# Sums and splits of two x pairs interleaved in the first feed-forward periods, sums of steady periods moved, one query product made a filler

## The chip, the cores and the metric

The kernel runs on one core of a Trainium2 chip. The metric is the device time in microseconds of one execution of the whole program. Three executions of the kernel before gave 1489.28, 1490.77 and 1493.35 us; the median is 1490.77 us. PE stands for TensorE (matmuls), DVE for VectorE, ACT for ScalarE, POOL for GpSimd and SP for SyncE.

## The reference

The program is a two-layer encoder trunk over 512 frames and 16 meta tokens, of width 1024. Each layer is a mixer (retention in the first, latent attention in the second) and a SwiGLU feed-forward of hidden width 2816. What the change touches are the two feed-forwards and the query products of the second layer. Cut to that, the reference is:

```python
def swiglu(hn, w1, w3, w2):
    return (jax.nn.silu(hn @ w1) * (hn @ w3)) @ w2
...
    cq = rmsnorm(hn @ w_q_a, q_a_norm_g)
    q = (cq @ w_q_b).reshape(B, L, MLA_HEADS, MLA_NOPE + MLA_ROPE)
    ...
        sc = jnp.einsum('bqhd,bkhd->bhqk', q[:, s:e], k[:, :e])
...
    for layer in range(DEPTH):
        h = h + mixer(rmsnorm(h, norm_mix_g[layer]))
        h = h + swiglu(rmsnorm(h, norm_ffn_g[layer]), ffn_w1[layer], ffn_w3[layer], ffn_w2[layer])
    return rmsnorm(h, final_g)[:, PAD + N_META:]
```

All inputs are float32, and so is the result. Numbers are carried as a high and a low part: every 128-wide matmul step is three matmuls (high by high, high by low, low by high).

## The kernel before

**Splits.** `split(hi, lo, z)` (its two instructions are recorded at L335 and L331) is an ACT cast that writes the high part and a DVE subtraction that writes the low part. The subtraction reads what the cast wrote, so DVE cannot begin it before ACT has ended. Weights arrive by DMA in a tile `raw` and are split into `whi` and `wlo`; operands are split into `xp`. All plain DVE additions and subtractions are recorded at L331 too.

**The feed-forward.** `ffn(0, True)` works on 528 columns (two halves of w = 264), `ffn(1, False)` on 512 (two of 256). Both call `quads` (L812), which runs a list of *quads* in *periods*: eight `Up` quads (columns of w1 and w3), four `Down` quads (w2), then 6, 4, 8, 4 and 4. A quad is a 2x2 block product. Most quads are *mixed*: they take a Strassen-like scheme of seven products Q1 to Q7 instead of eight, each of four 128-wide steps, 12 matmuls. That needs sums and differences of the weight blocks (by DMAs that add while they write, `add1` and `add3` from POOL's queue, and by DVE, `sum2` and `sum4`) and of the operand blocks (four DVE operations `e<-e` in `operands`, L784). The first quads of each list (PLAIN = two in the first feed-forward, three in the second) and the last four are *plain*: eight products without any such sums, so they can start before the operands' sums exist.

**A mixed period** of quad q, with the next quad nxt and the one before prev, issues in this order (L909 to L995): product Q1; the split of group 2 of q's weights; an ACT copy of Q1's bank (L944); the hidden work of this period; Q7, Q3 and the recombination of prev; prev's evacuation `mid` (two DVE products `t<-a,r` and `t<-b,r`); `sum2(nxt)`, a DVE operation at L854; the split of q's third group; `sum4(nxt)`, a DVE subtraction `raw<-raw`; Q5; the split of group 1 of nxt, whose parts Q1 and Q5 of the next period read; Q2 and Q6; prev's SiLU on ACT; Q4 of prev; prev's `fin` on DVE. At the end of `quads` each engine's instructions are tied in this written order, so no scheduler changes it.

**Operands.** For the hidden units, `operands` runs in two half-steps, one per period (`hidden`, L1065): splits of three blocks and then the four `e<-e` in the first, the split of the four summed blocks `xp<-e,xp` in the second. A pair of `Up` quads makes one such operand, so a first half-step falls in every second period (a *heavy* one) and a second half-step in the periods between (*light* ones). For the four pairs of the input x, the first half-step runs with the mixer's last products (`prep_ffn`), and the rest, sums and split together, is in `self.sums`: a table `also` (L1039) says at which place of which period each runs. A place is a period and either "start", a number k (after the k-th step of period 0), "group2", "group1" or "end".

**The norm.** The feed-forward's RMS norm is applied after the first products. `root` (L1019) sums squares over partitions with two matmuls by ones (one for each half of the columns) into two free banks and takes their square roots on ACT (L1023); `inverse` (L1026) is a DVE reciprocal; `negated` (L1029) an ACT copy with the sign changed. `early` is `root` into the banks a1 and b1 of the second period. In the second feed-forward `squares` also makes the squares there (ACT) and their sum (DVE, `acc<-acc,t`).

**The second mixer** is placed by a scheduler from the program's order. The queries of each head are a product of 18 matmuls `query(n)` (L373) with a split after it; heads go through `scores`, `weights` and `values`, and between them a `Filler` runs as many pieces of other products as the table FILL says. Before the loop `query(0)` and `query(1)` are run to the end.

The main parts of the table and the loop:

```python
        drain(query(0))
        drain(query(1))
...
            cur.scores(0)
            filler.steps(FILL[n][0])
```

Of the kernel before, what the change touches and what calls it, by code (L numbers as in the profile page):

```python
# [52 lines left out]
A11, A21, A12, A22 = range(7, 11)  # L53
# [2 lines left out]
         "final": (40, 8), "kva": (48, 4), "qa": (52, 6), "gn": (58, 16)}  # L56
NG = 74

FILL = ((0, 0, 2, 1, 2), (2, 0, 2, 0, 1), (1, 0, 2, 2, 1), (1, 0, 1, 1, 2),
        (0, 1, 1, 1, 2), (1, 1, 1, 1, 2), (0, 1, 2, 2, 2), (0, 1, 0, 2, 2))  # L60


def drain(steps):
    for _ in steps:
        pass
# [195 lines left out]
class Kernel:  # L261
# [522 lines left out]
    def operands(self, pool, vv, w, b12=None):  # L784


        xp = pool.tile([P, 7, 2, HT], F32R, tag="xp", name=self.name("xp"))
        (b11, b12_), (b21, b22) = ((vv[:, i, :w], vv[:, i, w : 2 * w]) for i in range(2))
        for q, z in ((slice(Q1, Q3), vv[:, :, :w]), (Q3, b22)):
            self.split(xp[:, q, 0, :w], xp[:, q, 1, :w], z)  # L790
        if b12 is not None:
            self.split(*b12, b12_)
            yield xp
        self.tt(b11, b11, b12_, ALU.subtract)
        self.tt(b12_, b22, b12_, ALU.subtract)
        self.tt(b22, b22, b11, ALU.add)
        self.tt(b21, b22, b21, ALU.subtract)
        if b12 is None:
            yield xp
        self.split(xp[:, Q5:, 0, :w], xp[:, Q5:, 1, :w], self.blocks(vv, w))  # L800

    @staticmethod
# [9 lines left out]
    def quads(self, seq, first, w, ready, also, hidden):  # L812
# [3 lines left out]
        nc = self.nc  # L816
# [11 lines left out]
        def load1(q):  # L828
            q.r1 = f3(q, raw(q))
            nc.sync.dma_start(out=q.r1, in_=f3(q, q.src[:, : 2 * q.n]))  # L830
# [26 lines left out]
        def sum4(q):  # L857
            self.tt(q.r3[:, 1], q.r2[:, 1], q.r2[:, 0], ALU.subtract)
# [26 lines left out]
                    nc.tensor.matmul(bank, wt[u][:, cs], xp[:, p, v, :w], start=first and k == 0 and i == 0,  # L885
                                     stop=False, skip_group_check=True)

        def plain(q, j, k, rows=(0, 1)):

            cs = slice(k * P, (k + 1) * P)  # L890
            x1, x2 = q.blocks(k)[2 * j : 2 * j + 2]
            for row in rows:
                wt, banks = q.f[((A11, A12), (A21, A22))[row][j]], ((q.a, q.b), (q.d, q.c))[row]
                for bank, x in zip(banks, (x1, x2)):
                    for i, (u, v) in enumerate(((0, 0), (0, 1), (1, 0))):
                        nc.tensor.matmul(bank, wt[u][:, cs], x[v], start=j == 0 and k == 0 and i == 0,  # L896
                                         stop=False, skip_group_check=True)

        def begin():
            a, b = seq[:2]  # L900
# [8 lines left out]
        def period(i):  # L909
# [23 lines left out]
            if mixed(q):  # L933
                product(q, q.a, Q1, True)
            elif nxt:
                for k in pairs:
                    plain(q, 0, k)
            if q:
                group2(q)
                on("group2")  # L940
# [11 lines left out]
            if mixed(prev):  # L952
                product(prev, prev.d, Q7, False)
                product(prev, prev.b, Q3, False)
                combine(prev)
            prev.mid(prev.a, prev.b)
            if mixed(nxt):
                sum2(nxt)
            if mixed(q):
                group(q, q.r3, Q7, Q3)  # L960
            if mixed(far):
                load3(far)
            if mixed(nxt):
                sum4(nxt)
            if mixed(q):
                product(q, q.c, Q5, True)
            elif nxt:
                for k in pairs:
                    plain(q, 1, k)
            else:  # L970
                for row in range(2):
                    for k in pairs:
                        plain(q, 0, k, (row,))
                        plain(q, 1, k, (row,))
            if mixed(q):
                q.q5 = self.temp()[:, :w]
                nc.scalar.copy(out=q.q5, in_=q.c)
            if nxt:
                group1(nxt)
                if far:  # L980
                    load2(far)
                if i >= first - 1 and i + 3 < len(seq):
                    load1(seq[i + 3])
            on("group1")
            if mixed(q):
                product(q, q.a, Q2, False)
# [21 lines left out]
    def ffn(self, layer, full):  # L1008
# [25 lines left out]
                self.square_add(acc, self.h[k][:, META:], k == 0)  # L1034


        sums = [partial(drain, z) for z in self.sums]
        early = partial(root, (self.banks[1][0], self.banks[1][1][:, 0]))
        if full:  # L1039
            also = {(0, "start"): [sums[0]], (0, 1): [early, sums[1]], (0, 3): [inverse],  # L1040
                    (1, "group1"): [sums[2]], (1, "end"): [sums[3], negated]}
        else:
            also = {(0, "start"): [squares, sums[0]], (0, 3): [early], (1, "group2"): [inverse],
                    (1, "group1"): [sums[1]], (1, "end"): [negated], (2, "group1"): [sums[2]],
                    (2, "end"): [sums[3]]}

# [36 lines left out]
    def mla(self):  # L1085
# [83 lines left out]
        def query(n):  # L1169
            def evac(m, ps):  # L1170
                hi, lo = self.slot(F32R), self.slot(F32R)
                self.split(hi[:, :SEQ], lo[:, :SEQ], ps[:, :SEQ])
                qn[n] = hi, lo

            yield from self.gemm(a["w_qbn"], n, 1, cq, False, evac=evac)
# [35 lines left out]
        drain(rotary(0))  # L1211
        drain(second)
        drain(query(0))
        drain(query(1))


        order = {"q2": query(2), "q3": query(3), "r1": rotary(1), "q4": query(4), "kv2": keys_values(2), "p0": project([0], 0), "p0b": project([0], 1), "q5": query(5), "q6": query(6), "kv3": keys_values(3), "q7": query(7), "p1": project([1], 0), "p1b": project([1], 1), "p2": project([2], 0), "p2b": project([2], 1)}
        filler = Filler(order)
        prev = None
        for n in range(MH):  # L1220
# [177 lines left out]
```

## Time and profile before

| what | value |
|---|---|
| median of three executions | 1490.77 us (1489.28 to 1493.35) |
| the profiled execution | 1495.9 us |
| span of its trace, first to last instruction | 1494.1 us |
| PE busy | 1430.9 us, 96% of the span |
| DVE busy | 1135.4 us, 76% |
| ACT busy | 738.1 us, 49% |
| POOL busy | 129.8 us, 9% |
| mean granted PE clock | 0.986 |
| moved by DMA | 176.8 MB, 118 GB/s over the span |

A busy share is a mean over stages with different limits. In this profile PE is idle for some 63 us of the span, so that what is to be looked at is in which places PE waits, for whom, and at which clock it goes on. [...] The rows that matter are in the section after the next one.

### The profile page before, as it was taken

Reading aid. Unit: us, or ns where it says so; the run is one execution under the profiler, and the core shown is the slowest. Engines: PE = TensorE matmul, PEld = TensorE weight load, DVE = VectorE, ACT = ScalarE, POOL = GpSimd, SP = SyncE. Lnnn points to the kernel's source line nnn. Section 1 sums busy time; section 2 is a strip of 40 time slices with the busy share of each in tenths; the row PEclk is TensorE's granted clock in tenths of the full one; section 3 lists DMA queues with packets and bytes.
Section 4 is the critical chain, followed back from the end, with each engine's and each line's share of the span. In section 5 each row is a group of like instructions: output and inputs, shape, how many; then the busy total and the mean of one; then the engine's idle time right before and its main releaser. Section 6 shows DMA issues by size and latency. Waiting matters only on the chain.

```text
span 1494.1 us, 27739 instructions
## 1 busy us (share of the span) xinstructions
PE 1430.9 (96%) x11088; PEld 1384.1 (93%) x11088; DVE 1135.4 (76%) x1823; ACT 738.1 (49%) x1299; POOL 129.8 (9%) x170
## 2 busy tenths in 40 slices
PE   8999999999999799999999999999998899999995
PEld 8999999999999799999999989788888899999995
DVE  8675565565578898988987777667887998989876
ACT  5452342442446555555554535655563555545542
POOL 2000000000000111111110000100000111111100
PEclk9999999999999999999999999999999999999997
DMA  6213213213122667768764332411114667677741
GB/s 220 85 52 105 79 47 112 62 53 114 59 65 78 160 156 191 178 161 200 170 155 119 100 95 72 118 45 54 57 57 110 150 166 195 160 187 186 165 130 64
DMA packets 77314, 176.80 MB, mean 118 GB/s; under 512 B 8944, under 2 KB 24432, under 8 KB 77184
## 3 DMA queue, kind: packets, MB, share of 16 engines
q1 hardware_dynamic: 56592, 138.76, 30.0%
q0 software_dynamic: 20592, 36.26, 14.2%
q8 instruction: 87, 1.43, 0.4%
q14 instruction: 43, 0.35, 0.1%
HBM read 171.57 MB, written 2.10 MB: 116 GB/s over the span
## 4 chain that ended last, share of the span: by engine, by line
PE 74%; DVE 15%; issue 4%; DMA 4%; ACT 3%; POOL 0%; DVEq 0%; ACTq 0%; POOLq 0%
PE ps L371 19%; PE b L885 19%; PE ps L373 8%; PE a L885 8%; PE ps L638 7%; DVE wlo L331 4%; PE b L896 3%; DMA raw<-w 2%; PE ps L721 2%; DVE e L331 2%; PE ps L679 2%; PE ps L116 1%; DVE xp L331 1%; DVE raw L331 1%; DVE t L331 1%
## 5 line engine op out<-in xcount | busy, mean ns | idle before, releaser
L335 ACT CAST whi<-raw 128x1024 fp32r<-128x1024 f32 (+4 forms) x402 | 347.6, 869 | 294.9 <-PE ps L371 136.9
L885 PE MATMUL b<-xp,whi 128*128 128x264 f32 (+1 forms) x2280 | 417.9, 283 | 13.0 <-ACT b L944 7.4
L331 DVE TENSOR_TENSOR wlo<-raw,whi 128x1024 fp32r<-128x1024 f32 (+4 forms) x402 | 395.8, 994 | 43.1 <-ACT whi L335 40.6
L885 PEld LDWEIGHTS b<-xp,whi 128*128 128x128 f32 x2280 | 353.1, 189 | 13.4 <-ACT b L944 13.4
L885 PE MATMUL b<-xp,wlo 128*128 128x264 f32 (+1 forms) x1140 | 322.9, 283 | 0.0
L371 PE MATMUL ps<-s,whi 128*128 128x264 f32 x1824 | 301.8, 288 | 8.2 <-ACT whi L335 6.7
L371 PEld LDWEIGHTS ps<-s,whi 128*128 128x128 f32 x1824 | 256.2, 191 | 10.6 <-ACT whi L335 6.8
L885 PEld LDWEIGHTS b<-xp,wlo 128*128 128x128 f32 x1140 | 215.4, 189 | 0.0
L371 PE MATMUL ps<-s,wlo 128*128 128x264 f32 x912 | 186.8, 286 | 0.0
L885 PE MATMUL a<-xp,whi 128*128 128x264 f32 (+1 forms) x912 | 171.5, 284 | 0.6 <-ACT whi L335 0.6
L885 PE MATMUL a<-xp,wlo 128*128 128x264 f32 (+1 forms) x456 | 131.5, 288 | 12.1 <-DVE wlo L331 12.0
L371 PEld LDWEIGHTS ps<-s,wlo 128*128 128x128 f32 x912 | 142.8, 190 | 0.1
L885 PEld LDWEIGHTS a<-xp,whi 128*128 128x128 f32 x912 | 141.4, 189 | 0.8 <-ACT whi L335 0.8
L848 POOL DMA_DIRECT2D raw<-w x63 | 54.6, 867 | 842.9 <-DMA raw<-w 351.8
L373 PE MATMUL ps<-s,whi 128*128 128x512 f32 x368 | 119.1, 405 | 3.4 <-ACT t L127 3.4
L638 PE MATMUL ps<-whi,s 128*128 128x256 f32 x640 | 116.5, 282 | 0.3 <-DVE s L331 0.3
L885 PEld LDWEIGHTS a<-xp,wlo 128*128 128x128 f32 x456 | 86.0, 189 | 17.3 <-DVE wlo L331 17.2
L638 PEld LDWEIGHTS ps<-whi,s 128*128 128x128 f32 x640 | 99.1, 188 | 0.6 <-PE ps L118 0.3
L331 DVE TENSOR_TENSOR s<-ps,s 128x256 fp32r<-128x256 f32 (+3 forms) x88 | 46.5, 545 | 65.2 <-ACT s L335 50.8
L638 PE MATMUL ps<-wlo,s 128*128 128x256 f32 x320 | 89.5, 280 | 0.0
L373 PEld LDWEIGHTS ps<-s,whi 128*128 128x128 f32 x368 | 68.7, 192 | 18.2 <-ACT t L127 3.5
L335 ACT CAST xp<-e 128x528 fp32r<-128x528 f32 (+5 forms) x82 | 56.2, 717 | 42.3 <-DVE e L331 42.2
(178 smaller groups left out, 2104.9 us busy)
## 6 DMA issues: line engine op xcount, KB each, us to landing
raw<-w SPq DMA_DIRECT2D x133, 256.0 KB, 3.9
raw<-w SPq DMA_DIRECT2D x49, 512.0 KB, 5.2
raw<-w POOLq DMA_DIRECT2D x78, 256.0 KB, 5.4
raw<-w SPq DMA_DIRECT2D x72, 192.0 KB, 2.9
raw<-w SPq DMA_DIRECT2D x24, 384.0 KB, 4.1
raw<-w POOLq DMA_DIRECT2D x48, 192.0 KB, 4.1
raw<-w_v SPq DMA_DIRECT2D x16, 512.0 KB, 3.8
raw<-w_g SPq DMA_DIRECT2D x16, 512.0 KB, 3.5
```

Of the source, the lines that this page charges most:

```text
L116: nc.tensor.matmul(out, x[:, qs], y[:, cs], start=t == 0, stop=t == 4 and not masked)
L331: self.nc.vector.tensor_tensor(out=out, in0=a, in1=b, op=op)
L335: self.nc.scalar.copy(out=hi, in_=src)
L371: mm(ps[:, h * 512 : h * 512 + HT], w[p], x[q][:, h * HT : (h + 1) * HT], start=s, stop=e)
L373: mm(ps[:, :SEQ], w[p], x[q], start=s, stop=e)
L638: mm(ps[:, :256], x[k][p][:, c], w[k][q], start=k == 0 and i == 0, stop=k == last and i == 2)
L679: nc.tensor.matmul(ps[:n, half * 512 : half * 512 + HT], k[d][p][:, t0 : t0 + n], q[d][s][:, half * HT : (half + 1) * HT], start=i == 0, s ...
L721: mm(out, v[j][p][:, c], s[:, c0 : c0 + HT], start=j == 0 and i == 0, stop=False)
L848: nc.gpsimd.dma_start(out=q.r1[:, 1], in_=q.part(3), accum_op=ALU.add)
L885: nc.tensor.matmul(bank, wt[u][:, cs], xp[:, p, v, :w], start=first and k == 0 and i == 0, stop=False, skip_group_check=True)
L896: nc.tensor.matmul(bank, wt[u][:, cs], x[v], start=j == 0 and k == 0 and i == 0, stop=False, skip_group_check=True)
```

## The change

The change has six parts.

1. `operands`: in steady periods two of the four `e<-e` stay in the first half-step and the other two go to the second half-step, directly ahead of its ACT cast. For pairs of x there is now a stop between the four sums and the split, so that `also` can place them apart (`add` and `split` in place of `sums`).
2. `also`: sums and splits of the x pairs are set at other places, those of two pairs interleaved. In the first feed-forward the sums of pairs 0 and 1 both run before the split of pair 0, and pair 2's sums go after `mid` of period 1 (a new place "mid"). In the second one pair 0's sums follow `early`, its split is in period 1, and the others move along; `negated` moves to a later period in both.
3. `early` in the second feed-forward puts both halves' sums into the bank a1, one half beside the other, where they went into a1 and b1.
4. `plain` takes a list of banks. In period 1 all steps of one bank come before the next bank, in the order (0, 1), (1, 0), (1, 1), (0, 0): bank a, which the root uses, is last. Before, all four banks were served step by step.
5. `sum4(nxt)` moves from before Q5 to behind the split of group 1 of nxt, in every period with a mixed nxt.
6. `query(1)` is no longer run to the end before the loop; it is the first piece of the filler, taken after the first scores of head 0 (FILL's first entry is 1 where it was 0).

```diff
-FILL = ((0, 0, 2, 1, 2), (2, 0, 2, 0, 1), (1, 0, 2, 2, 1), (1, 0, 1, 1, 2),
+FILL = ((1, 0, 2, 1, 2), (2, 0, 2, 0, 1), (1, 0, 2, 2, 1), (1, 0, 1, 1, 2),
...
         self.tt(b11, b11, b12_, ALU.subtract)
         self.tt(b12_, b22, b12_, ALU.subtract)
+        if b12 is None:
+            yield xp
         self.tt(b22, b22, b11, ALU.add)
         self.tt(b21, b22, b21, ALU.subtract)
-        if b12 is None:
-            yield xp
+        if b12 is not None:
+            yield
         self.split(xp[:, Q5:, 0, :w], xp[:, Q5:, 1, :w], self.blocks(vv, w))
...
-        def plain(q, j, k, rows=(0, 1)):
+        def plain(q, j, k, of=((0, 0), (0, 1), (1, 0), (1, 1))):
...
-                for k in pairs:
-                    plain(q, 0, k)
+
+                for of in ((0, 1), (1, 0), (1, 1), (0, 0)) if i == 1 else ((0, 0), (0, 1), (1, 0), (1, 1)):
+                    for k in pairs:
+                        plain(q, 0, k, (of,))
...
             prev.mid(prev.a, prev.b)
+            on("mid")
             if mixed(nxt):
                 sum2(nxt)
             if mixed(q):
                 group(q, q.r3, Q7, Q3)
             if mixed(far):
                 load3(far)
-            if mixed(nxt):
-                sum4(nxt)
             if mixed(q):
                 product(q, q.c, Q5, True)
...
+            if mixed(nxt):
+                sum4(nxt)
             on("group1")
...
-        sums = [partial(drain, z) for z in self.sums]
-        early = partial(root, (self.banks[1][0], self.banks[1][1][:, 0]))
+        add, split = ([partial(f, z) for z in self.sums] for f in (next, drain))
+        a1, b1 = self.banks[1]
+        early = partial(root, (a1, b1[:, 0]) if full else (a1[:, :w], a1[:, w:]))
         if full:
-            also = {(0, "start"): [sums[0]], (0, 1): [early, sums[1]], (0, 3): [inverse],
-                    (1, "group1"): [sums[2]], (1, "end"): [sums[3], negated]}
+            also = {(0, "start"): [add[0], add[1], split[0]], (0, 1): [early, split[1]], (0, 3): [inverse],
+                    (1, "mid"): [add[2]], (1, "group1"): [add[3], split[2]], (1, "end"): [split[3]],
+                    (2, "group1"): [negated]}
         else:
-            also = {(0, "start"): [squares, sums[0]], (0, 3): [early], (1, "group2"): [inverse],
-                    (1, "group1"): [sums[1]], (1, "end"): [negated], (2, "group1"): [sums[2]],
-                    (2, "end"): [sums[3]]}
+            also = {(0, "start"): [squares], (0, 3): [early, add[0]], (1, "group2"): [split[0], inverse],
+                    (1, "group1"): [add[1]], (1, "end"): [split[1]], (2, "mid"): [add[2]],
+                    (2, "group1"): [add[3], split[2]], (2, "end"): [split[3]], (3, "group1"): [negated]}
...
-        drain(query(1))
...
-        order = {"q2": query(2), "q3": query(3), "r1": rotary(1), "q4": query(4), "kv2": keys_values(2), "p0": project([0], 0), "p0b": project([0], 1), "q5": query(5), "q6": query(6), "kv3": keys_values(3), "q7": query(7), "p1": project([1], 0), "p1b": project([1], 1), "p2": project([2], 0), "p2b": project([2], 1)}
+        order = {"q1": query(1), "q2": query(2), "q3": query(3), "r1": rotary(1), "q4": query(4),
```

**Place 1: DVE, first feed-forward, period 1, from its `mid` on.** `e_5249` and `e_5329` are the third and fourth x pair, `xp_5284` and `xp_5364` their split operands, `raw_5396<-raw_5387` is `sum2` and `raw_5394<-raw_5396` is `sum4` of the first mixed quad. Before:

```order
L331 TENSOR_TENSOR t_5567<-a_0_5376,r 128x264
L331 TENSOR_TENSOR t_5567<-b_0_5377,r 128x264
L854 SCALAR_TENSOR_TENSOR raw_5396<-raw_5387 128x512
L331 TENSOR_TENSOR raw_5394<-raw_5396 128x512
L331 TENSOR_TENSOR wlo_5623<-raw_5387,whi_5622 128x1024
L331 TENSOR_TENSOR e_5249<-e_5249 128x264 x4
L331 TENSOR_TENSOR xp_5284<-e_5249,xp_5284 128x4x264
L331 TENSOR_TENSOR t_5637<-b_0_5377,t_5567 128x528
L331 TENSOR_TENSOR e_5639<-t_5637,r 128x528
L331 TENSOR_TENSOR e_5329<-e_5329 128x264 x4
L331 TENSOR_TENSOR xp_5364<-e_5329,xp_5364 128x4x264
L331 TENSOR_TENSOR wlo_5662<-raw_5396,whi_5661 128x1024
```

Now:

```order
L331 TENSOR_TENSOR t_5567<-a_0_5376,r 128x264
L331 TENSOR_TENSOR t_5567<-b_0_5377,r 128x264
L331 TENSOR_TENSOR e_5249<-e_5249 128x264 x4
L856 SCALAR_TENSOR_TENSOR raw_5396<-raw_5387 128x512
L331 TENSOR_TENSOR wlo_5626<-raw_5387,whi_5625 128x1024
L331 TENSOR_TENSOR raw_5394<-raw_5396 128x512
L331 TENSOR_TENSOR e_5329<-e_5329 128x264 x4
L331 TENSOR_TENSOR xp_5284<-e_5249,xp_5284 128x4x264
L331 TENSOR_TENSOR t_5641<-b_0_5377,t_5567 128x528
L331 TENSOR_TENSOR e_5643<-t_5641,r 128x528
L331 TENSOR_TENSOR xp_5364<-e_5329,xp_5364 128x4x264
L331 TENSOR_TENSOR wlo_5661<-raw_5396,whi_5660 128x1024
```

The third pair's sums now come first and the fourth pair's stand between them and the third pair's split, and `sum4` stands behind the low weights of group 1.

**Place 2: DVE, second feed-forward, period 3 (the first mixed quad), from the split of the last x pair to the low weights of the next quad's group 1.** `xp_12766` is that split, `e_13047` the first hidden pair, `raw_1801` is `sum2` and `raw_1798` is `sum4` of the next quad; the last `wlo` row belongs to that quad's group 1. Before:

```order
L331 TENSOR_TENSOR xp_12766<-e_12755,xp_12766 128x4x256
L331 TENSOR_TENSOR wlo_13201<-raw_13038,whi_13200 128x1024
L331 TENSOR_TENSOR xp_13208<-e_13049,xp_13208 128x2x256
L331 TENSOR_TENSOR xp_13208<-e_13049,xp_13208 128x256
L331 TENSOR_TENSOR e_13049<-e_13049 128x256 x4
L331 TENSOR_TENSOR t_13217<-a_1_12778,r 128x256
L331 TENSOR_TENSOR t_13217<-b_1_12779,r 128x256
L854 SCALAR_TENSOR_TENSOR raw_1801_13167<-raw_1796_13105 128x512
L331 TENSOR_TENSOR wlo_13222<-raw_12984,whi_13221 128x1024
L331 TENSOR_TENSOR raw_1798_13112<-raw_1801_13167 128x512
L331 TENSOR_TENSOR wlo_13243<-raw_1796_13105,whi_13242 128x1024
```

Now:

```order
L331 TENSOR_TENSOR xp_12766<-e_12755,xp_12766 128x4x256
L331 TENSOR_TENSOR wlo_13200<-raw_13038,whi_13199 128x1024
L331 TENSOR_TENSOR xp_13207<-e_13047,xp_13207 128x2x256
L331 TENSOR_TENSOR xp_13207<-e_13047,xp_13207 128x256
L331 TENSOR_TENSOR e_13047<-e_13047 128x256 x2
L331 TENSOR_TENSOR t_13214<-a_1_12778,r 128x256
L331 TENSOR_TENSOR t_13214<-b_1_12779,r 128x256
L856 SCALAR_TENSOR_TENSOR raw_1801_13169<-raw_1796_13104 128x512
L331 TENSOR_TENSOR wlo_13219<-raw_12984,whi_13218 128x1024
L331 TENSOR_TENSOR wlo_13239<-raw_1796_13104,whi_13238 128x1024
L331 TENSOR_TENSOR raw_1798_13115<-raw_1801_13169 128x512
```

Two of the four sums of the hidden pair have left this stretch (they come back one period later, just ahead of that pair's second split), and `sum4` stands behind the low weights where it stood ahead of them.

**Place 3: PE, second mixer, the end of head 0's query product (`ps_10773`) and what follows.** `ps_10802` is head 1's query product before and head 0's first scores (L116) now, for which `ps_10816` is head 1's query product; `s_10798` is the high part of head 0's queries and `s_10799` the low part. Before:

```order
L373 MATMUL ps_10773<-s_10596,whi_10775 128x512
L373 MATMUL ps_10773<-s_10597,whi_10775 128x512
L373 MATMUL ps_10773<-s_10596,wlo_10776 128x512
L373 MATMUL ps_10802<-s_10507,whi_10804 128x512
L373 MATMUL ps_10802<-s_10508,whi_10804 128x512
L373 MATMUL ps_10802<-s_10507,wlo_10805 128x512
L373 MATMUL ps_10802<-s_10512,whi_10804 128x512
```

Now:

```order
L373 MATMUL ps_10773<-s_10597,whi_10775 128x512
L373 MATMUL ps_10773<-s_10596,wlo_10776 128x512
L116 MATMUL ps_10802<-s_10383,s_10798 128x256
L116 MATMUL ps_10802<-s_10384,s_10798 128x256
L373 MATMUL ps_10816<-s_10507,whi_10818 128x512
L373 MATMUL ps_10816<-s_10508,whi_10818 128x512
L373 MATMUL ps_10816<-s_10507,wlo_10819 128x512
L116 MATMUL ps_10802<-s_10383,s_10799 128x256
L116 MATMUL ps_10802<-s_10172,s_10675 128x256
L116 MATMUL ps_10802<-s_10173,s_10675 128x256
L118 LDWEIGHTS ma
L118 MATMUL ps_10802<-mb,ma 128x64
```

Where 18 matmuls of head 1's query product followed head 0's at once, the first two matmuls of the scores now stand between them, with the high part of head 0's queries as their input; 15 of the 18 come behind the scores.

## Rows read from the trace of the kernel before

**Rows 1.** Page, part 1: busy us, share of the span, instructions of each engine.

```profile
PE 1430.9 (96%) x11088; PEld 1384.1 (93%) x11088; DVE 1135.4 (76%) x1823; ACT 738.1 (49%) x1299; POOL 129.8 (9%) x170
```

**Rows 2.** Waits of PE over the whole span: total us, times, longest us.

```profile
PE a L885 <- DVE wlo L331: 12.0, 20, 1.9
```

**Rows 3.** Timeline of PE, single rows: start, us, operation, [idle before <- releaser].

```profile
498.85 0.59 PE L885 MATMUL b<-xp,whi 128*128 128x264 f32 x1 [7.41 <-ACT b L944]
...
517.12 0.39 PE L885 MATMUL a<-xp,wlo 128*128 128x264 f32 x1 [1.28 <-DVE wlo L331]
...
1130.58 0.39 PE L896 MATMUL a<-xp,whi 128*128 128x256 f32 x1 [3.44 <-ACT r L1023]
...
1162.09 0.58 PE L885 MATMUL b<-xp,whi 128*128 128x256 f32 x1 [5.56 <-DVE xp L331]
...
1170.06 0.38 PE L885 MATMUL a<-xp,wlo 128*128 128x256 f32 x1 [1.86 <-DVE wlo L331]
```

**Rows 4.** Stretches: us, then busy us (instructions) of each engine, PEclk, DMA share.

```profile
496.14:502.97 6.83, 4.12 (x19) 4.13 (x19) 5.50 (x7) 4.66 (x7) 0.00 (x0) 0.50 0.23 59
1130.60:1134.40 3.80, 3.80 (x19) 3.80 (x20) 2.54 (x2) 2.17 (x3) 0.00 (x0) 0.56 0.06 17
1162.00:1166.00 4.00, 3.91 (x21) 3.91 (x22) 3.90 (x9) 2.73 (x6) 0.00 (x0) 0.61 0.23 66
1170.10:1175.00 4.90, 4.90 (x42) 4.90 (x43) 4.60 (x6) 2.60 (x4) 0.00 (x0) 1.00 0.70 199
937.10:941.20 4.10, 4.10 (x19) 3.36 (x19) 3.40 (x6) 2.86 (x5) 0.00 (x0) 1.00 0.29 94
518.65:539.75 21.10, 20.75 (x170) 20.53 (x169) 19.72 (x30) 12.11 (x20) 3.44 (x4) 1.00 0.74 177
1171.55:1192.15 20.60, 20.03 (x170) 19.82 (x169) 19.48 (x30) 11.99 (x20) 3.44 (x4) 1.00 0.77 174
```

**Rows 5.** Timeline of DVE, first feed-forward, periods 0 and 1.

```profile
478.07 3.45 DVE L1027 RECIPROCAL r<-r 128x528 f32<-128x528 f32 x1
...
486.07 0.69 DVE L331 TENSOR_TENSOR raw<-raw 128x512 f32<-128x512 f32 x1 [2.20 <-DMA raw<-w]
...
490.78 1.26 DVE L331 TENSOR_TENSOR xp<-e,xp 128x1056 fp32r<-128x1056 f32 x1 [1.14 <-ACT xp L335]
...
497.07 1.26 DVE L331 TENSOR_TENSOR xp<-e,xp 128x1056 fp32r<-128x1056 f32 x1 [1.14 <-ACT xp L335]
```

**Rows 6.** Timeline of POOL's queue, same place.

```profile
489.33 0.86 POOL L848 DMA_DIRECT2D raw<-w  x1 [14.90 <-PE a L896]
```

**Rows 7.** DMA issues from 480 to 500 us: count, KB, median us to landing.

```profile
raw<-w POOLq DMA_DIRECT2D x3, 256.0 KB, 6.5
```

**Rows 8.** Timeline of ACT, second feed-forward, around the root.

```profile
1127.69 1.04 ACT L335 CAST xp<-e 128x1024 fp32r<-128x1024 f32 x1 [4.55 <-DVE e L331]
1128.76 1.28 ACT L1023 ACT_TABLE_LOAD   x1
...
1130.42 0.47 ACT L1023 ACTIVATE r<-b,eps_rms 128x256 f32<-128x256 f32 x1
```

**Rows 9.** Waits of DVE from 1125.8 to 1163.1 us.

```profile
DVE xp L331 <- ACT xp L335: 4.5, 4, 1.1
DVE raw L331 <- DMA raw<-w: 3.8, 1, 3.8
DVE wlo L331 <- ACT whi L335: 1.9, 1, 1.9
```

**Rows 10.** Timeline of DVE, second feed-forward, period 3.

```profile
1163.13 1.02 DVE L331 TENSOR_TENSOR xp<-e,xp 128x512 fp32r<-128x512 f32 x2
1164.07 1.80 DVE L331 TENSOR_TENSOR e<-e 128x256 f32<-128x256 f32 x4
```

**Rows 11.** Timeline of ACT, second mixer: high part of head 0's queries.

```profile
938.69 0.59 ACT L335 CAST s<-ps 128x512 fp32r<-128x512 f32 x1
```

**Rows 12.** Waits of DVE over the whole span.

```profile
DVE raw L854 <- DMA raw<-w: 5.0, 3, 2.4
```

More of the change, by code (lines that the diff above doesn't have):

```diff
@@ L886, in product @@
                                      stop=False, skip_group_check=True)
-        def plain(q, j, k, rows=(0, 1)):
+        def plain(q, j, k, of=((0, 0), (0, 1), (1, 0), (1, 1))):
             cs = slice(k * P, (k + 1) * P)
[L891 to L897, printed above, removed]
+            xs = q.blocks(k)[2 * j : 2 * j + 2]
+            for row, col in of:
+                wt, x = q.f[((A11, A12), (A21, A22))[row][j]], xs[col]
+                bank = ((q.a, q.b), (q.d, q.c))[row][col]
+                for i, (u, v) in enumerate(((0, 0), (0, 1), (1, 0))):
+                    nc.tensor.matmul(bank, wt[u][:, cs], x[v], start=j == 0 and k == 0 and i == 0,
+                                     stop=False, skip_group_check=True)
         def begin():
@@ L972, in period @@
                     for k in pairs:
-                        plain(q, 0, k, (row,))
-                        plain(q, 1, k, (row,))
+                        for j in range(2):
+                            plain(q, j, k, ((row, 0), (row, 1)))
             if mixed(q):
@@ L1213, in mla @@
         drain(query(0))
-        drain(query(1))
-        order = {"q2": query(2), "q3": query(3), "r1": rotary(1), "q4": query(4), "kv2": keys_values(2), "p0": project([0], 0), "p0b": project([0], 1), "q5": query(5), "q6": query(6), "kv3": keys_values(3), "q7": query(7), "p1": project([1], 0), "p1b": project([1], 1), "p2": project([2], 0), "p2b": project([2], 1)}
+        order = {"q1": query(1), "q2": query(2), "q3": query(3), "r1": rotary(1), "q4": query(4),
+                 "kv2": keys_values(2), "p0": project([0], 0), "p0b": project([0], 1), "q5": query(5),
+                 "q6": query(6), "kv3": keys_values(3), "q7": query(7), "p1": project([1], 0),
+                 "p1b": project([1], 1), "p2": project([2], 0), "p2b": project([2], 1)}
         filler = Filler(order)
```

## The prediction

> **What bounds the kernel now.** I read the page's busy shares first, then the waits of PE, then the places of the long ones with the clock behind them, and last DVE and ACT there. PE is busy 1430.9 of 1494.1 us [rows 1], so the time is PE's work plus the 63 us in which it stands idle plus what slow clocks add. The changed places hold these gaps: 7.41 us at 498.85 and 1.28 at 517.12 in the first feed-forward, 3.44 at 1130.58, 5.56 at 1162.09 and 1.86 at 1170.06 in the second [rows 3]. [...] The rest of the edited code is small waits for weights' low parts, 20 times 12.0 us with the 1.28 and the 1.86 among them [rows 2]. In all these places DVE or ACT is late, and DVE itself is held up by casts and transfers. So the question is how many of DVE's waits the new order covers.
>
> **First feed-forward, periods 0 to 3.** From the reciprocal (478.07) to the end of the last split of x (497.07 + 1.26 = 498.33) pass 20.3 us, of which DVE waits 2.20 for a transfer and twice 1.14 for a cast that it had itself released the moment before [rows 5]. That leaves 15.8 us of work, and the change does the same operations in another order. With sums of another pair, or `sum4` and a weight split, ahead of each reader, I count all three waits as covered: other DVE work of 1.8 and more stands in each. The reciprocal comes about 1.0 earlier (an estimate: one wait like the 1.14, ahead of it, is covered by the second pair's sums). So the last split ends at 477.1 + 15.8 = 492.9 instead of 498.3. PE was free at 498.85 - 7.41 = 491.4. The copy ahead of Q5 (I allow 0.3 for it) no longer sits behind ACT's late casts, and only Q5's last three matmuls read the last split: nine matmuls of 20.75/170 = 0.122 us [rows 4] are 1.1, so they come up at 492.9 too. The gap goes, 7.1 us. With it goes the slow stretch: 4.12 us busy at half clock lose 2.06. The 1.28 at 517.12 falls too. What is late next is the weights' sum: an accumulating transfer issued on POOL's queue at 489.33, released by PE work that is not moved [rows 6], lands 6.5 later [rows 7], at 495.8 or a little earlier; then DVE needs `sum2` and two low splits, some 2.9 (0.6, and 1.15 each by the 1.26 of a slightly larger split [rows 5]), to 498.7 at the latest. PE, with Q5, Q2 and Q6 (36 matmuls, 4.4) done, asks for it at 496.4. A new wait of 1.5 to 2.3; I take 2.0. Sum: -7.1 - 2.06 - 1.28 + 2.0 = **-8.4**. If none of DVE's waits were covered, only the second casts' time would be won, about -1; if the transfer landed 2 earlier, -10.4.
>
> **Second feed-forward, periods 0 to 4.** Before the root ACT stands idle for 4.55 us, waiting for DVE's sums of pair 0; then come the cast, 1.28 of table load and the square roots [rows 8], and PE waits 3.44. Now the cast is behind the root, so the table load falls into the idle time. The two halves share a bank, so the second sum is tied behind the first root: that costs about its 0.47 [rows 8] but holds only bank a, and PE goes on with bank b, which needs neither. DVE, from 1125.8 on, waits 4.5 + 3.8 + 1.9 = 10.2 us for casts, a transfer and weights [rows 9] before the hidden pair's first split at 1163.13 [rows 10]. With the same operations and no wait that row would come at 1152.9. A third of the transfer's 3.8 I keep, 1.3, because transfers start when PE and DVE free their tiles: 1154.2. From there to the weights for which PE waits until 1170.06 were 6.9 us of DVE work. Half of the four sums (1.80, so 0.9) and `sum4` (0.6, the 0.69 of rows 5 with its overlap) leave this stretch: 5.4, so 1159.6. PE could be there at 1156.5: Q5 at 1162.09 less the 5.56 and the 3.44, less 1.67 of slow clock after the first gap (3.80 x 0.44) with the 0.47 given back, is 1151.9; then 6.1 us of products less 1.5 of slow clock (3.91 x 0.39). DVE is the later one, so the whole is 1170.06 - 1159.6 = **-10.4**, and a wait of 3.1 is left at that point, larger than the 1.86. That is nearer to 3.44, behind which the clock fell, than to 1.86, behind which it stayed; so I add **+1.6**, the mean of 1.67 and 1.5. Bounds: with no wait of DVE left -11.8 and no drop; with every wait kept only the 1.5 us of moved work is won.
>
> **Steady periods.** `sum4` stood ahead of the low weights for which PE waits, and is now behind them. It counts where DVE reaches `sum2` late because of its transfer, which is 3 times, 5.0 us [rows 12]: 3 x 0.6 = **-1.8**. In the other places, 18 small waits of 12.0 - 1.28 - 1.86 = 8.9 us in all, it can win up to 0.4 each. Against that stands the new half-step: two sums directly ahead of the cast that reads them. The nearest rows are the 1.14 [rows 5], and there are nine such pairs in each layer. A pair's two periods take 21.10 us with PE busy 20.75 and DVE 19.72, and 20.60 with PE 20.03 and DVE 19.48 in the second feed-forward [rows 4]. DVE plus 1.14 is 20.86 and 20.62: no more than the pair takes now. I count it at nothing. The cover is DVE's idle 1.38 and 1.12; where that is gone the 1.14 is added in full. The small waits I take as unmoved; bounds -7 and +20.5 (18 x 1.14).
>
> [...]
>
> **Second mixer.** The first scores read the high part of head 0's queries, an ACT cast at 938.69 that lasts 0.59 [rows 11]. PE began head 1's product at 937.1 and had 4.10 us without a gap [rows 4]. Now two matmuls of the scores stand ahead of it, and PE must wait for the cast from 937.2 to 939.3: **+2.1**. The cover was that product. No gap nearby is shortened in return, and later rows of this part are in the same order. Bounds: 0 if the cast comes at once, since the order of ACT ahead of it could close up, and +3.8 with a clock drop.
>
> **Sum.** -8.4 - 10.4 + 1.6 - 1.8 + 2.1 = -16.9 us. The profiled execution took 1495.9 us (span 1494.1 and 1.8 around it), 5.1 above the median of 1490.77; the difference is applied to the median: **1473.9 us** (and 1479.0 for an execution like the profiled one).
>
> **The rivals.**
> - *Transfers hold the first periods.* The 2.20 [rows 5] and all of the 3.8 [rows 9] stay, because loads keep their old times. +2.2 and +2.5, less what the later waits shrink by: about 1477. For it: DVE is faster, the transfers are not. Against: in part their buffers are freed earlier.
> - *The clock falls behind the new gaps as well*, of 2.0 in the first feed-forward and 2.1 in the mixer, between the 1.86 that kept it and the 3.44 that did not. +2.06 + 1.7: about 1477.7.
> - *More is covered:* the second feed-forward has no transfer wait and no drop, and the small waits give 3: -1.3 - 1.6 - 3, about 1468.
> - *It doesn't do what it says in period 2:* the copy ahead of Q5 still queues behind casts on ACT, and the 7.1 and 2.06 stay: 1483.
> - *Other side, slower than before:* the cast's 1.14 reaches PE in all 18 pairs. 20.5 - 16.9 = +3.6, so 1494.4. For it: DVE's idle time in a pair includes waits for PE that cannot be given up, and 1.12 of cover against 1.14 is thin. It decides from the point where a pair's DVE work plus the wait is above 21.1 or 20.6 us.
>
> **How the numbers follow.** Forecast 0.55 (its own range 1471 to 1477), transfers 0.13, clock 0.12, more covered 0.10, copy 0.04, casts 0.06. The range 1467.5 to 1480 leaves out the last two and some tail. What a measurement can tell from no change is about 0.3%, 4.5 us, so faster is below 1486.3 and slower above 1495.2. The casts' case lies around that upper line and gives half to each: faster 0.93, same 0.04, slower 0.03.
>
> **What would show it.** The gaps of 7.41, 3.44 and 5.56 are gone; a wait for low weights of about 2 near 496 and one of about 3 near 1157 with 0.5 clock behind it; a gap of 2.1 ahead of the first scores; DVE with some 18 more waits of 1.1 for `xp`; pairs of periods still near 21.1 and 20.6. A pair above 22 would prove the last rival, a gap ahead of Q5 released by the copy the one before.

## The result, and the profile after

The changed kernel takes 1475.89 us (median of 4 runs, 1473.63 to 1477.33), the kernel before on the same chip 1491.76. The ratio is 0.9892, 95% interval 0.9875 to 0.9909: about 15.9 us less. The forecast was 16.9 less. The profiled execution of the changed kernel took 1473.63 us, span 1471.9. It lies 2.3 below its median and the one of before lay 4.1 above its own, so the two traces are 22 us apart where the medians are 16.

Part 1 of the profile's page of the changed kernel (beside [rows 1]), and its waits of PE (beside [rows 2]; line numbers have moved by 2 to 5):

```profile
PE 1422.8 (97%) x11088; PEld 1376.7 (94%) x11088; DVE 1131.2 (77%) x1823; ACT 736.9 (50%) x1299; POOL 129.7 (9%) x170
```

```profile
PE a L887 <- DVE wlo L331: 8.0, 17, 1.6
PE b L887 <- DVE xp L331: 3.6, 4, 0.9
PE ps L116 <- ACT s L335: 2.1, 1, 2.1
PE b L887 <- ACT xp L335: 1.2, 4, 0.3
PE b L887 <- ACT b L948: 0.9, 2, 0.5
PE a L1027 <- ACT r L1028: 0.6, 1, 0.6
```

The waits for low weights are 8.0 us where they were 12.0. The four waits for DVE's `xp` (3.6) and four for ACT's (1.2) are new, and so is the 2.1 for ACT's `s`. The long gaps of [rows 3] are gone; what stands at their places, in the timeline of PE of the changed kernel:

```profile
492.33 0.51 PE L887 MATMUL b<-xp,whi 128*128 128x264 f32 x2 [0.45 <-ACT b L948]
...
518.30 0.39 PE L887 MATMUL a<-xp,wlo 128*128 128x264 f32 x1 [0.60 <-DVE wlo L331]
...
928.61 0.50 PE L116 MATMUL ps<-s,s 128*128 128x256 f32 x2 [2.06 <-ACT s L335]
...
1118.33 0.48 PE L1027 MATMUL a<-acc,ones 128*128 128x256 f32 x1 [0.57 <-ACT r L1028]
...
1149.97 0.38 PE L887 MATMUL a<-xp,wlo 128*128 128x256 f32 x1 [1.56 <-DVE wlo L331]
```

There is 0.45 where 7.41 stood and nothing like the wait of 2.0 near 496. The 1.28 at the third mixed quad is gone; the 0.60 stands one quad later, where the kernel before shows no such wait. PE waits 2.06 ahead of the first scores, 0.57 at the root in place of 3.44, and 1.56 where 1.86 stood and 3.1 was forecast. The 5.56 is gone.

The ACT copy of Q1's bank comes once in every mixed period, so it dates the same event in both traces. Four of them, before (L944):

```profile
518.65 0.36 ACT L944 COPY b<-a 128x264 f32<-128x264 f32 x1 [2.56 <-PE a L885]
...
793.31 0.36 ACT L944 COPY b<-a 128x264 f32<-128x264 f32 x1 [1.03 <-PE a L885]
...
1161.68 0.36 ACT L944 COPY b<-a 128x256 f32<-128x256 f32 x1
...
1442.88 0.36 ACT L944 COPY b<-a 128x256 f32<-128x256 f32 x1 [0.96 <-PE a L885]
```

and after (L948):

```profile
508.73 0.36 ACT L948 COPY b<-a 128x264 f32<-128x264 f32 x1 [1.01 <-PE a L887]
...
785.62 0.36 ACT L948 COPY b<-a 128x264 f32<-128x264 f32 x1 [1.03 <-PE a L887]
...
1143.26 0.36 ACT L948 COPY b<-a 128x256 f32<-128x256 f32 x1 [1.31 <-PE a L887]
...
1422.36 0.36 ACT L948 COPY b<-a 128x256 f32<-128x256 f32 x1 [0.96 <-PE a L887]
```

The first (third mixed quad of the first feed-forward) comes 9.9 us earlier, the second (its last mixed quad) 7.7, the third (first mixed quad of the second feed-forward) 18.4, the last 20.5. So 2.2 us are *lost* in the steady periods of the first feed-forward, and the second one's, measured from its second mixed quad on (1171.55 before, 1151.46 after), win 0.4.

### The profile page after: what moved, and what is told of

It is laid out like the page before. It is cut to its first block, busy times and chain, and to the rows that moved or that the text cites. A ratio compares the mean times of both kernels' runs of the same rounds, so it can differ in the third digit from the quotient of the medians.

```text
span 1471.9 us, 27735 instructions
## 1 busy us (share of the span) xinstructions
PE 1422.8 (97%) x11088; PEld 1376.7 (94%) x11088; DVE 1131.2 (77%) x1823; ACT 736.9 (50%) x1299; POOL 129.7 (9%) x170
## 3 DMA queue, kind: packets, MB, share of 16 engines
q0 software_dynamic: 20592, 36.26, 14.1%
## 4 chain that ended last, share of the span: by engine, by line
PE 73%; DVE 18%; ACT 3%; issue 3%; DMA 2%; DVEq 0%; ACTq 0%; POOLq 0%
PE ps L371 22%; PE b L887 16%; PE ps L373 8%; DVE wlo L331 7%; PE ps L638 6%; PE a L887 6%; PE b L898 4%; PE ps L721 2%; DVE xp L331 2%; DVE t L331 2%; DVE e L331 2%; PE ps L679 2%; PE ps L116 2%; DMA raw<-w 1%; ACT xp L335 1%
## 5 line engine op out<-in xcount | busy, mean ns | idle before, releaser
L331 DVE TENSOR_TENSOR wlo<-raw,whi 128x1024 fp32r<-128x1024 f32 (+4 forms) x402 | 389.9, 995 | 40.1 <-ACT whi L335 37.3
L331 DVE TENSOR_TENSOR xp<-e,xp 128x528 fp32r<-128x528 f32 (+5 forms) x82 | 64.1, 808 | 22.9 <-ACT xp L335 22.7
```

The lines of the kernel that those rows point to most:

```text
L331: self.nc.vector.tensor_tensor(out=out, in0=a, in1=b, op=op)
```

## The experiments

Differences between traces are read at these copies, so they leave out the scatter of whole runs; medians go beside them. "Changed" is the changed kernel. The runs are on three chips, each with its own runs of the kernel before: the first four with a median of 1494.41 us, the next four with 1493.34, the last two with 1493.63.

**The yardstick.** No edit.

> The changed kernel once more, beside the three kernels below on the same chip, as the yardstick for differences of 2 to 7 us. Expected: ratio to the kernel before 0.9892 as before (0.9875 to 0.9909), 2.06 us of wait of PE ahead of the first scores, and at each of the four passages from Up to Down quads two gaps of 0.25 to 0.33 and 0.87 to 0.91. The low clock at the start of the second mixer (half level from 830.65 to 837.48 in the trace before, not there in the trace after) is open: if the order of the matmuls there decides it, it is absent again; if it is chance, it may come back and cost about 2 us.

Measured: 1475.88 us, ratio 0.9878 (0.9855 to 0.9901), before 1494.41. The waits are those named. The low clock near 830 (PEclk, the granted share of full speed: 0.50 from 830.65 to 837.48 in the kernel before, 1.00 from 820 to 840 in the first trace of changed) came back for half the time, 3.4 us from 823.4 on where it was 6.8 before; the mean granted clock is 0.992, in the first trace of changed 0.994. The same kernel shows it once and once not, so it is chance at least in part, and I count it as no term of the change.

**Head 1's query product put back.**

```diff
+        drain(query(1))
...
-        order = {"q1": query(1), "q2": query(2), ...
+        order = {"q2": query(2), ...
```

> The changed kernel with head 1's query product ahead of the first scores again. Theory: the 2.06 us wait ahead of the first scores is this move's price and nothing later gives it back, so 2.1 us less than the changed kernel, with no gap above 0.1 us there. Rival: the part of the mixer up to the 3.36 us wait for ACT near 960 is set by ACT, not by PE, so that wait grows by the same 2 us and the time stays.

Measured: 1473.14 us, ratio 0.986 (0.9836 to 0.9884), 2.7 less than the yardstick. The wait ahead of the first scores is gone, and the one for ACT further on is what it was, in the waits of PE of this kernel:

```profile
PE ps L373 <- ACT t L127: 3.4, 1, 3.4
```

So it did not grow by 2, and the rival falls: the move cost its 2.1 us. (The 2.7 of the medians would not show it by itself, since the runs overlap.) The two traces are 3.4 apart at the end of the mixer; the rest goes with a low-clock stretch behind that wait, 3.4 us long here and 6.8 in the yardstick (mean granted clock 0.993 and 0.992).

**The moved sums of steady pairs put back.**

```diff
-        if b12 is None:
-            yield xp
         self.tt(b22, b22, b11, ALU.add)
         self.tt(b21, b22, b21, ALU.subtract)
-        if b12 is not None:
-            yield
+        yield xp
```

> The changed kernel with all four sums of a steady pair in the first half-step again. Theory: the moved sums cost 1.7 us at each of the four passages from Up to Down, since there the split comes behind the cast's 1.14 us and the 0.9 of two sums while the first Down quad's Q5 waits for it, and they win only about 0.1 for each of some 14 other pairs; so the time is 6.8 - 1.4 = 5.4 us less than the changed kernel's. Rival: the moved sums carry the gain of the steady pairs (0.6 a pair, 14 pairs): 8.4 - 6.8 = 1.6 us more.

Measured: 1465.42 us, ratio 0.981 (0.9784 to 0.9835): 10.5 less than the yardstick, 9.7 at the last copy, where I had expected 5.4. The four passages give 1.67 to 1.75 each, as expected. But each steady pair wins too, 0.53 in the first feed-forward and about 0.5 in the second, where I had expected to lose 0.1. Waits of PE of this kernel:

```profile
PE a L884 <- DVE wlo L331: 4.6, 4, 2.6
PE a L884 <- ACT whi L335: 0.5, 1, 0.5
```

The 17 waits of 8.0 us have become 4 of 4.6, though one has grown, from 1.56 to 2.64 at the second mixed quad of the second feed-forward; and where Up quads follow Down quads there, PE now waits 1.16 and the 0.5 of the second row.

**sum4 put back** ahead of Q5.

```diff
             if mixed(far):
                 load3(far)
+            if mixed(nxt):
+                sum4(nxt)
             if mixed(q):
                 product(q, q.c, Q5, True)
...
-            if mixed(nxt):
-                sum4(nxt)
             on("group1")
```

> The changed kernel with sum4 ahead of Q5 again, before the low weights of group 1. Theory of the prediction: only the places where DVE reaches sum2 late because of its transfer count, 3 times 0.6, so 1.8 us more than the changed kernel. Rival: the low weights set PE's start in all steady periods, and each of the waits of 0.26 to 0.47 (some 14 of them) grows by 0.6: 8 to 10 us more.

Measured: 1490.88 us, ratio 0.9979 (0.9965 to 0.9994): 15 more than the yardstick, 13.1 at the last copy. Its waits of PE:

```profile
PE a L887 <- DVE wlo L331: 19.0, 22, 2.8
```

22 waits of 19.0 us. Between the copies the loss is 0.58 to 0.63 in every second steady period, and 1.7 and 1.8 at the first mixed quads. The rival's mechanism is right, though its 8 to 10 was too low, and my term of 1.8 is wrong.

**The first feed-forward's table put back.**

```diff
-            also = {(0, "start"): [add[0], add[1], split[0]], (0, 1): [early, split[1]], (0, 3): [inverse],
-                    (1, "mid"): [add[2]], (1, "group1"): [add[3], split[2]], (1, "end"): [split[3]],
-                    (2, "group1"): [negated]}
+            also = {(0, "start"): [add[0], split[0]], (0, 1): [early, add[1], split[1]], (0, 3): [inverse],
+                    (1, "group1"): [add[2], split[2]], (1, "end"): [add[3], split[3], negated]}
```

> The changed kernel with the first feed-forward's table of places as before; everything else of the change stays. The changed kernel reaches the third quad's Q1 copy 9.9 us earlier than the kernel before, and 1.8 of that came back when sum4 was put back. Theory: the other 8.1 are the table's, so about 8 us more than the changed kernel, with a gap of some 5 to 7 us ahead of the first Q5 and half clock behind it. Rival: sum4 and the bank order made the gain and the table little: under 3 us more.

Measured: 1483.52 us, ratio 0.9937 (0.992 to 0.9955): 7.6 more than the yardstick. At the third mixed quad's copy it is 9.0 us behind the yardstick and 8.6 behind the first trace of changed, at the last copy of this feed-forward 8.9 and 8.6. The gap is back, in its timeline of PE:

```profile
498.32 0.59 PE L887 MATMUL b<-xp,whi 128*128 128x264 f32 x1 [6.57 <-ACT b L948]
```

**The second feed-forward's table, root and order of banks put back.** The edit is the diff's `else` branch, `early` and the order of banks undone for that layer. It is not the step-by-step order of before, as the expectation calls it: the loop of the changed kernel stays, and all steps of one bank still come before the next.

> The changed kernel with the second feed-forward's table of places, its root in two banks and the step-by-step order of period 1 as before; everything else of the change stays. Theory: 11 us were won from the root to the second mixed quad, of which 1.8 belong to sum4 and about 2.5 to the two sums moved out of the first hidden pair; the table and the root are worth the other 7, so about 7 us more, with the gaps of 3.4 and 5 us back. Rival: DVE's waits only move elsewhere and under 3 us come back.

Measured: 1483.54 us, ratio 0.9937 (0.9919 to 0.9955); 6.9 us behind the yardstick at the first mixed quad, 5.1 at the end, since the yardstick loses 1.7 once near 1320. From the root's sums to the second mixed quad's copy it takes 42.93, against 34.39 and 34.81 in the two traces of changed, so 8.1 to 8.5 more. Both gaps are back:

```profile
1121.68 0.50 PE L898 MATMUL a<-xp,whi 128*128 128x256 f32 x2 [3.45 <-ACT r L1028]
...
1152.09 0.50 PE L887 MATMUL b<-xp,whi 128*128 128x256 f32 x2 [4.38 <-ACT b L948]
```

**Only the root and the order of banks put back**, the table kept; here too the banks stay one behind the other.

```diff
-        early = partial(root, (a1, b1[:, 0]) if full else (a1[:, :w], a1[:, w:]))
+        early = partial(root, (a1, b1[:, 0]))
...
-                for of in ((0, 1), (1, 0), (1, 1), (0, 0)) if i == 1 else ((0, 0), ...
+                for of in ((0, 1), (1, 0), (1, 1), (0, 0)) if i == 1 and w == HT else ((0, 0), ...
```

> The changed kernel with only the second feed-forward's root in two banks and the step-by-step order of period 1 put back; its table of places stays. Theory of the prediction: what removed the 3.44 us wait behind the root is that the cast stands behind the root now, so the table load falls into idle time; the bank only adds the 0.57 us for the second sum and hides the square root. So within 1 us of the changed kernel, a wait of 0.5 to 1.2 us after the sums instead of the 0.57. Rival: the bank order is what removed it: 3 us or more.

Measured: 1477.08 us, ratio 0.9893 (0.9879 to 0.9908), the same as the changed kernel's 0.9878 to 0.9892. Its timeline of ACT shows the table load ahead of the root's sums, and ACT ready and waiting for PE:

```profile
1118.24 1.28 ACT L1028 ACT_TABLE_LOAD   x1
...
1121.48 0.47 ACT L1028 ACTIVATE r<-a,eps_rms 128x256 f32<-128x256 f32 x1 [1.95 <-PE a L1027]
```

The square roots follow the sums at once, and PE waits 0.13, less than the 0.5 to 1.2 that I expected. Putting the cast behind the root removed the 3.44; the shared bank and the order of banks are worth nothing that shows.

That the banks are served one behind the other was undone in no run by itself. The loop does it for the first half of every plain quad that comes after period 0 and has another quad behind it, not only in period 1. In the kernel before there stand four waits of 0.43 in the last plain quads of both layers:

```profile
PE b L896 <- DVE h L331: 1.7, 4, 0.4
```

They are in the three kernels with the old loop (before, and the last two below) and in no other. Each other part of the change is undone in one of those without them, so the new loop is what removes them.

**A version from these findings:** query product put back, steady sums put back save for the first hidden pair of the second feed-forward.

```diff
+                one = len(ops) < sum(PARTS[:3]) and (full or len(ops) > 0)
-                rest.append(make(room[len(ops)][0], hid[len(ops)], w))
+                rest.append(make(room[len(ops)][0], hid[len(ops)], w, **({"whole": True} if one else {})))
```

> The changed kernel with two parts taken out: head 1's query product is run ahead of the first scores as before, and all four sums of a steady pair stand in the first half-step as before, save for the first pair of the second feed-forward, where two sums stay moved because the next wait there grew by 2.5 us without that. Theory: 2.1 less for the query product, 9.7 less for the pairs and 2.5 less for the exception, so about 1462 us and faster than both kernels. Rival: with PE earlier the transfers become the limit (a wait of 1.2 and a clock drop did appear near the second passage back to Up quads), and half of it is lost: about 1468.

Measured: 1459.48 us, ratio 0.9776 (0.9759 to 0.9792): faster than both kernels, 33.9 us below the kernel before. Part 1 of its page, and its waits for low weights:

```profile
PE 1417.5 (97%) x11088; PEld 1375.2 (95%) x11088; DVE 1131.6 (78%) x1823; ACT 739.5 (51%) x1299; POOL 130.0 (9%) x170
```

```profile
PE a L889 <- DVE wlo L331: 3.4, 5, 1.5
```

**One part alone, in the kernel before: sum4.** The edit is that of the diff.

> The kernel before with one part of the change alone: sum4 behind the split of group 1. The prediction gave this part 3 x 0.6 = 1.8 us, for the places where a transfer is late. Theory now: in every second steady period PE waits for these low weights (18 waits, 8.9 us, besides the 1.28 and the 1.86), and sum4's 0.6 stands in front of each, so nearly all of the small waits go: 7 to 9 us less than the kernel before. Rival: the step of the prediction, 1.8 us less.

Measured: 1475.86 us, ratio 0.9883 (0.9866 to 0.99). This one edit is worth as much as the whole change, 17.8 us, and twice what I expected even then. Of the 17.6 by which its last copy is earlier, 12.9 lie in the steady periods, 1.7 and 1.9 at the first mixed quads of the two layers, and 1.0 around the second mixer. Its waits of PE, its stretch from the third copy to the fifth (columns as in [rows 4]) and its DVE there:

```profile
PE a L885 <- DVE wlo L331: 2.9, 4, 1.1
```

```profile
516.92:537.40 20.48, 20.48 (x170) 20.48 (x169) 19.53 (x30) 12.12 (x20) 3.45 (x4) 1.00 0.76 185
```

```profile
522.03 2.35 DVE L331 TENSOR_TENSOR wlo<-raw,whi 128x1024 fp32r<-128x1024 f32 x2
...
524.30 0.68 DVE L331 TENSOR_TENSOR raw<-raw 128x512 f32<-128x512 f32 x1
```

`sum4` runs behind the two low splits. A pair takes 20.48 where it took 21.10 [rows 4], and PE is busy in all of it. So the 20.75 that I had read as PE's need held 0.27 of waiting. In the pair before, one matmul starts 0.64 after the one ahead of it and the next 0.23 later, where 0.12 is usual; each is drawn some 0.28 long, so only 0.35 of that shows as a gap. The 0.35 and the 0.27 make the 0.6.

**One part alone, in the kernel before: the moved sums.**

> The kernel before with one part of the change alone: two of the four sums of a steady pair one half-step later, ahead of the cast. The prediction gave this part nothing, since a pair's DVE work and the 1.14 fit into the time of the pair. Theory now: it costs 1.7 us at each of four passages from Up to Down and some 0.1 in each of 14 other pairs (the same 0.6 of waiting either way while sum4 stands ahead of the low weights): 7 to 9 us more than the kernel before, slower. Rival: 0 to 2 us more.

Measured: 1507.71 us, ratio 1.0091 (1.0074 to 1.0107): 14.1 us slower, where I had expected 7 to 9. Its waits of PE, the pair from the third copy to the fifth, and DVE in it:

```profile
PE a L885 <- DVE wlo L331: 19.9, 22, 1.7
PE b L885 <- DVE xp L331: 9.1, 5, 5.5
```

```profile
517.67:539.07 21.40, 20.73 (x170) 20.51 (x169) 19.41 (x30) 12.06 (x19) 3.45 (x4) 1.00 0.73 173
```

```profile
519.22 0.89 DVE L331 TENSOR_TENSOR e<-e 128x264 f32<-128x264 f32 x2
...
521.25 1.26 DVE L331 TENSOR_TENSOR xp<-e,xp 128x1056 fp32r<-128x1056 f32 x1 [1.14 <-ACT xp L335]
```

The 1.14 ahead of the split is there as forecast. A light period (split of the second half-step) gets 0.9 to 1.35 longer, the heavy one that gave up two sums only 0.6 to 0.9 shorter, so a pair loses about 0.5 and the four passages 1.7 each. By the copies the steady periods lose 17.0 together; 2.9 come back at the first mixed quads and around the second mixer. Why DVE's idle time was no cover shows in the kernel before, in the same pair (timeline of DVE):

```profile
520.56 1.26 DVE L331 TENSOR_TENSOR xp<-e,xp 128x1056 fp32r<-128x1056 f32 x1 [0.28 <-ACT xp L335]
...
527.48 0.71 DVE L331 TENSOR_TENSOR t<-b,t 128x528 f32<-128x528 f32 x1 [0.90 <-PE b L885]
```

Its larger idle piece, 0.90, lies at the products behind Q6, after the low weights for which PE waits. Work put ahead of those weights cannot use it.

## Why the prediction was right

The change came out 1.0 us smaller than forecast, and in both feed-forwards for the causes that the prediction names. That the sum is so close is luck.

Between the two traces the first feed-forward won 9.9 (forecast 8.4) and the second 11.2 (8.8); the steady periods lost 1.8 (forecast: won 1.8) and the second mixer 2.1. That makes 17.2, with gains put 3.9 too low and the steady periods 3.6 too good. Inside the steady periods two terms were both wrong and nearly cancelled. The other 5 us between the two traces lie around the second mixer, where the 6.8 us at 0.50 near 830 are in one trace alone, and behind the last copy; the four waits of 0.43 stood in these places, and the prediction has no term for them.

As a check, the medians of the runs that undo single parts give 15.0, 7.6 and 7.7 won and 2.7 and 10.5 lost, 17.1 in all, beside the yardstick's 18.5.

- **First feed-forward, -8.4:** right in mechanism, low in size. The copy of the third mixed quad comes 9.9 earlier; the table gives 8.6 to 9.0 of it and `sum4` 1.7 (the two overlap). DVE waits nowhere from the reciprocal to the last split, and all three waits are covered, that for the transfer too (`sum2`, L856, at 493.97 begins without one):

```profile
477.51 3.45 DVE L1032 RECIPROCAL r<-r 128x528 f32<-128x528 f32 x1
...
488.46 1.25 DVE L331 TENSOR_TENSOR xp<-e,xp 128x1056 fp32r<-128x1056 f32 x1
...
490.99 1.25 DVE L331 TENSOR_TENSOR xp<-e,xp 128x1056 fp32r<-128x1056 f32 x1
...
493.97 0.68 DVE L856 SCALAR_TENSOR_TENSOR raw<-raw 128x512 f32<-128x512 f32 x1
494.57 2.35 DVE L331 TENSOR_TENSOR wlo<-raw,whi 128x1024 fp32r<-128x1024 f32 x2
```

The last split ends at 492.2 where I said 492.9, though the reciprocal came 0.6 earlier and not 1.0 (DVE still waits 1.35 for a cast ahead of it). The term that failed is the new wait of 2.0: the two low splits begin at 494.57, right behind `sum2`, so the transfer no longer sets them. That POOL's accumulating transfer keeps its old time was the wrong assumption: it was issued 1.6 earlier, and by the timeline what it waited for last was a landing and not PE:

```profile
487.73 0.86 POOL L850 DMA_DIRECT2D raw<-w  x1 [12.87 <-DMA raw<-w]
```

- **Second feed-forward, -10.4 + 1.6:** from the root's sums to the second mixed quad's copy 11.2 us were won. DVE waits 1.8 us in place of 10.2; I had kept 1.3. The wait left at the second mixed quad was 1.56, not 3.1: counted from the root's sums (1126.01 before, 1117.07 after) the low weights came 0.7 earlier and PE 0.85 later than forecast. The clock did not fall there (1.00 from 1149.97 to 1154.00), and the +1.6 was not due. `sum4`, which I counted out of this stretch as 0.6, gave 1.8. The causes hold: with the table put back both gaps return, and the bank and the order of banks alone do nothing that shows.
- **Steady periods, -1.8 + 0:** wrong twice. The step "it counts where DVE reaches `sum2` late because of its transfer, which is 3 times" failed: low weights are on PE's path in every second period, and `sum4` there is worth 0.6 each time, 13.1 us in the changed kernel and 17.8 alone. The step from DVE's work plus 1.14, "no more than the pair takes now", to "I count it at nothing" failed as well: 9.7 us in the changed kernel, 14.1 alone. (By its own numbers it did not hold in the second layer, 20.62 against 20.60.) Undone one at a time the two come to -3.4 in the changed kernel, of which 3.5 lie at the first mixed quads; between the kernel before and the changed one the steady periods proper lost 1.8, so the two parts do not simply add up.
- **The rival on the other side** (the cast's wait reaches PE in all 18 pairs, 20.5 us) had the mechanism and its reason right: DVE's 18 waits ahead of late splits came, 1.11 to 1.15 us each, and idle time that waits for PE (the 0.90 at 527.48 in the kernel before) cannot be given up. Its price was too high, since the heavy period gives 0.6 to 0.9 back, and it lost to a term that I had put at a tenth. At the four passages it shows bare, in DVE and in PE of the changed kernel:

```profile
552.48 0.89 DVE L331 TENSOR_TENSOR e<-e 128x264 f32<-128x264 f32 x2
...
554.51 1.26 DVE L331 TENSOR_TENSOR xp<-e,xp 128x1056 fp32r<-128x1056 f32 x1 [1.14 <-ACT xp L335]
```

```profile
554.53 0.39 PE L887 MATMUL b<-xp,whi 128*128 128x264 f32 x1 [0.25 <-ACT xp L335]
...
555.83 0.39 PE L887 MATMUL b<-xp,whi 128*128 128x264 f32 x1 [0.90 <-DVE xp L331]
```

The first Down quad's Q5 needs the pair that is being split, so 0.25 and 0.90 of PE's time go as gaps and the rest of the 1.67 stands in what is drawn as busy.
- **Second mixer, +2.1:** right, 2.06 measured, and nothing gave it back.
- **Clock rival:** behind the 2.06 the clock stayed at 1.00 in the changed kernel, from 928.61 to 932.50.

In these traces DVE idles the 1.14 ahead of the late splits at 521.25 and 554.51 (rows above), with other DVE work written behind them. With the sums that they follow, such waits cost 14.1 us in the kernel that has the moved sums alone.

## What to carry to other kernels

Ask of every operation on a feeding engine not whether that engine has idle time, but whether the operation stands ahead of or behind the result that the bounding engine waits for; the idle time must lie on the same side. In this kernel, moving a 0.6 us subtraction behind such a result was worth as much as the whole change, and moving two sums in front of one cost nearly as much. When several edits are bundled, undo each alone: here two of six parts were losses, and without them (save for the moved sums of one pair) the change wins 33.9 us instead of 15.9.

## What the runs showed of the hardware that I had not expected

PE's busy time held waiting: the same 170 matmuls show 20.75 us busy with a gap of 0.35 in 21.10, and 20.48 without a gap. The clock after a wait of 2 us is not decided by its length alone. Behind the wait of 2.06 ahead of the first scores it stayed at 1.00 in the changed kernel (a stretch as in [rows 4]):

```profile
928.61:932.50 3.89, 3.89 (x20) 3.28 (x21) 2.06 (x5) 2.35 (x4) 0.00 (x0) 1.00 0.59 190
```

In the kernel with the steady sums put back the same wait was 2.05, and the clock behind it fell to 0.50 for 3.4 us:

```profile
923.95:927.30 3.35, 3.35 (x12) 2.77 (x12) 1.94 (x4) 0.76 (x2) 0.00 (x0) 0.50 0.63 179
```

In the kernel with only the root and the order of banks put back, which is no different in this place, the wait was 2.06 and the clock fell as well, from 931.2 on for 3.4 us (mean granted clock of that execution 0.990, of the changed kernel's 0.994). So at this length both happen, and from these runs a forecast can give it a chance only.
